# A decoder layer on one core: the residual's transposes as a stream of their own through DRAM, and two output tiles of the next token group ahead of a group's queries

## The chip, the cores and the metric

The kernel runs on one core of a Trainium2 chip. The metric is the device time of one execution in microseconds (us); lower is better.

## What is computed

One inference step of a hybrid decoder layer with model width 1024, for a prompt of 1024 tokens and 8 sample tokens (each with its own state). Cut to what matters here:

```python
def layer(x, mem, ...):                      # x: 1024 prompt tokens, and 8 sample tokens
    h = rmsnorm(x, g_mix) @ w_in             # 1024 -> 2704
    gq, gk, gv, glr, gog, rx, ry, sq, sk, sv = split_cols(h)
    o_gla = gated linear attention of gq, gk, gv       # width 384
    hr    = rglru(causal_dwconv(rx))                   # width 384, a scan over the tokens
    o_rg  = hr * gelu(ry)
    o_swa = sliding window attention of sq, sk, sv     # width 256
    x = x + concat(o_gla, o_rg, o_swa) @ w_out         # 1024 -> 1024
    q = rmsnorm(rmsnorm(x, g_x) @ w_q)                 # 1024 -> 256, queries on the memory
    x = x + softmax(q mk^T / 8) mv @ w_o               # 256 memory rows; 256 -> 1024
    return x + square(relu(rmsnorm(x, g) @ w1)) @ w2   # 1024 -> 4096 -> 1024
```

## The kernel before

Everything lies with features on the 128 partitions and tokens along the free axis, so each product reads [128 x tokens] tiles. The 1032 tokens are three groups g of 344 columns. A float32 product is made of three products of a rounded high part and the rest (XH, XL for the activations, `wh`, `wl` for the weights), so one 128 x 344 output tile over 1024 inputs is 8 terms of 3, that is 24 matmuls. XH and XL hold eight blocks; when the mixer's three outputs are ready they stand there: gated linear attention in blocks 0 to 2, the recurrence in 3 to 5, window attention in 6 and 7.

**Stages.** "In" computes the first part of h (tiles q, k and v, with the memory's keys and values `mkv` between them), "mid" the rest of it (`win`), "mem" the output product (`wo`, 8 tiles per group), the queries (`wq`, 2 tiles per group), memory attention (`mx`, `mpt`, `mpo`) and its output product (`wmo`). After them, from about 760 us to the end, come the units of the feed-forward part.

**Streams.** The mixer and memory attention are Python generators (streams). While the main line of products is written out, a planner (`pump`) inserts steps of the streams that it holds ready, at a set share of TensorE time. A stream yields what it waits for: a flag such as ("ry", g), or a slot of a pool such as "e" (two tiles of 2064 columns). `pump(lambda: ...)` in `wout` writes steps of the streams until the group's mixer outputs are flagged. A scheduler then fixes the order on each engine, and each engine works its own order in sequence.

**Recurrence.** For each group: the gates (`rgp`, 18 matmuls in all for the last group), ScalarE and VectorE work, a scan on VectorE (L655). After the last scan VectorE copies the last states (`RT`), and TensorE transposes them (`rgtp`). `ry_gen` (L684) makes gelu(ry): it takes an "e" slot for `ru`, squares on GpSimd (L687, L688), multiplies on VectorE, takes a tanh on ScalarE, and after a flag from the scan multiplies with h and writes XH and XL. Its slot comes free only as the gates of the scan let theirs go.

**Weights.** They come in pieces of 512 columns into three `ws` buffers, all by the one queue of SyncE, are rounded by ScalarE (`wh`) and subtracted by VectorE (`wl`). `feed` keeps up to three pieces staged, across the steps known at that time; `run_steps()` writes out all steps gathered up to there, so a step behind it is not staged from ahead of it.

**Residual.** x comes from DRAM with tokens on the partitions, so it must be transposed: `residual` takes a tile of 128 tokens as two pieces in `ws` buffers, transposes it on TensorE (8 of 128 x 128 through the two `psB` banks, tile `xrp`, 72 in all), and copies the result into XT, in part by ScalarE (L160), in part by VectorE (L189). It stands on the main line: 32 transposes ahead of the first group's `wo`, 24 after it and 16 after the second group's. XT then takes the output product by an addition on VectorE (L170), and the sum of squares goes through `nrm` (matmuls with a matrix of ones), a logarithm and an exponential on ScalarE and a few VectorE steps into the factor by which `mq` scales `wq`.

## Time and profile before

| what | value |
|---|---|
| median of 3 runs | 1396.29 us (1394.62 to 1396.29) |
| the profiled execution | 1393.74 us |
| its span | 1392.0 us |
| mean granted TensorE clock | 0.984 of full |
| TensorE busy | 1332.0 us (96%) |
| VectorE, ScalarE, GpSimd busy | 992.3, 691.7, 260.1 us |

The three runs are whole executions; the profiled one is a fourth, and its span leaves out 1.74 us around the recorded instructions. A row of a timeline gives the start, the duration, the engine, the line and the operation with its output and inputs, and in brackets how long the engine sat idle before it and what ended that. Rows of one form that follow each other closely are put together (x8), with the time from the first start to the last end.

### The profile page before, as it was taken

The numbers are of one execution on the slowest core, as the hardware profiler recorded it, in microseconds if no ns is written. First come the engines' busy times: TensorE is split into PE (matmuls) and PEld (weight loads), VectorE is DVE, ScalarE is ACT, GpSimd is POOL, SyncE is SP. The second block draws the span as 40 slices with busy tenths as digits, with TensorE's granted clock in tenths as the row PEclk, the third lists the DMA queues.
The fourth block names the chain that finished last, engine by engine and source line by source line (L and its number), as shares of the span: only waits on it lengthen the run. The fifth ranks groups of instructions, "written<-read, shape, count | busy, mean of one in ns | idle before, by whom it ended". The sixth has DMA issues, their size and how long they took to land.

```text
span 1392.0 us, 23667 instructions
## 1 busy us (share of the span) xinstructions
PE 1332.0 (96%) x8675; PEld 1226.1 (88%) x8675; DVE 992.3 (71%) x2097; ACT 691.7 (50%) x1439; POOL 260.1 (19%) x245
## 2 busy tenths in 40 slices
PE   6999999999997989998999999999998999999998
PEld 5889888777876877786799999999998999999997
DVE  6276787668767664767698888888766666666674
ACT  5265455245476554555566776766663222222232
POOL 3001011300003101020004232243211321321310
PEclk9999999999998899999999999999999999999999
DMA  6114010211101444442243768766689867655403
GB/s 185 46 49 122 9 49 18 67 26 31 47 8 52 140 146 128 141 133 71 71 125 109 243 223 278 251 236 214 215 308 350 309 218 244 214 188 172 158 17 106
DMA packets 197499, 198.91 MB, mean 143 GB/s; under 512 B 27938, under 2 KB 177558, under 8 KB 197368
## 3 DMA queue, kind: packets, MB, share of 16 engines
q1 hardware_dynamic: 196744, 197.11, 43.7%
q8 instruction: 68, 1.11, 0.3%
q0 software_dynamic: 640, 0.30, 0.1%
q14 instruction: 47, 0.39, 0.1%
HBM read 136.83 MB, written 61.60 MB: 143 GB/s over the span
## 4 chain that ended last, share of the span: by engine, by line
PE 81%; DVE 10%; DMA 3%; ACT 3%; issue 1%; SPq 1%; POOL 1%; DVEq 0%; ACTq 0%; POOLq 0%
PE win L140 9%; PE e L140 9%; PE fe L140 8%; PE wo L140 6%; PE c L140 4%; PE d L140 4%; PE ga L140 4%; PE fa L140 4%; PE fd L140 4%; PE f L140 2%; PE v L140 2%; PE gx L140 2%; PE b L140 2%; PE fb L140 2%; PE fc L140 2%; PE fg L140 2%
## 5 line engine op out<-in xcount | busy, mean ns | idle before, releaser
L1906 POOL TENSOR_TENSOR wsum<-wraw 128x512 f32<-128x512 f32 x60 | 82.4, 1376 | 378.4 <-DVE wop L170 285.7
L140 PE MATMUL e<-XH,wop 128*128 128x344 f32 x512 | 133.3, 322 | 4.4 <-DVE XT L170 4.4
L160 ACT ACTIVATE wop<-wraw 128x512 fp32r<-128x512 f32 x120 | 74.4, 628 | 119.9 <-PE c L140 48.8
L140 PE MATMUL win<-XL,wh 128*128 128x344 f32 x384 | 126.6, 330 | 0.0
L140 PE MATMUL win<-XH,wh 128*128 128x344 f32 x384 | 126.1, 329 | 0.2 <-ACT xy L160 0.2
L140 PE MATMUL win<-XH,wl 128*128 128x344 f32 x384 | 125.5, 327 | 0.0
L160 ACT ACTIVATE wh<-ws 128x512 fp32r<-128x512 f32 x130 | 80.2, 628 | 74.7 <-DMA ws<-in_w_out_dram 21.2
L140 PE MATMUL fe<-XH,wop 128*128 128x344 f32 x448 | 114.7, 319 | 0.0
L170 DVE TENSOR_TENSOR wop<-wraw,wop 128x512 fp32r<-128x512 f32 x120 | 86.5, 721 | 38.1 <-ACT wop L160 37.1
L170 DVE TENSOR_TENSOR wl<-ws,wh 128x512 fp32r<-128x512 f32 x130 | 91.4, 715 | 27.2 <-ACT wh L160 21.8
L160 ACT ACTIVATE wop<-wsum 128x512 fp32r<-128x512 f32 x104 | 65.6, 631 | 84.7 <-PE e L140 59.0
L170 DVE TENSOR_TENSOR wop<-wsum,wop 128x512 fp32r<-128x512 f32 x104 | 74.5, 717 | 40.2 <-ACT wop L160 39.4
L140 PEld LDWEIGHTS e<-XH,wop 128*128 128x128 f32 x512 | 91.5, 190 | 4.7 <-issue 4.7
L140 PE MATMUL e<-XL,wop 128*128 128x344 f32 x256 | 82.5, 322 | 0.0
L140 PEld LDWEIGHTS fe<-XH,wop 128*128 128x128 f32 x448 | 78.9, 188 | 0.0
L140 PEld LDWEIGHTS win<-XL,wh 128*128 128x128 f32 x384 | 72.2, 188 | 5.2 <-issue 3.9
L140 PEld LDWEIGHTS win<-XH,wl 128*128 128x128 f32 x384 | 72.3, 188 | 3.6 <-issue 2.7
L140 PEld LDWEIGHTS win<-XH,wh 128*128 128x128 f32 x384 | 72.2, 188 | 3.3 <-issue 1.9
L140 PE MATMUL fe<-XL,wop 128*128 128x344 f32 x224 | 71.4, 319 | 0.0
L160 ACT ACTIVATE hc<-hc 128x344 f32<-128x344 f32 x126 | 61.4, 488 | 19.5 <-DVE hc L170 18.1
L170 DVE TENSOR_TENSOR hst<-hc,hst 128x344 fp32r<-128x344 f32 x79 | 60.5, 767 | 13.6 <-ACT hst L160 12.4
L140 PE MATMUL wo<-XH,wh 128*128 128x344 f32 x192 | 64.0, 334 | 2.5 <-ACT wh L160 2.5
(537 smaller groups left out, 3916.7 us busy)
## 6 DMA issues: line engine op xcount, KB each, us to landing
hd<-hst SPq DMA_DIRECT2D x90, 344.0 KB
wraw<-in_ffn_w_dram SPq DMA_DIRECT2D x60, 512.0 KB
hd<-wsum SPq DMA_DIRECT2D x54, 344.0 KB
XH<-hd SPq DMA_DIRECT2D x48, 344.0 KB
XL<-hd SPq DMA_DIRECT2D x48, 344.0 KB
xoph<-hd SPq DMA_DIRECT2D x24, 344.0 KB
xopl<-hd SPq DMA_DIRECT2D x24, 344.0 KB
ws<-in_w_in_dram SPq DMA_DIRECT2D x24, 256.0 KB
```

The costliest lines, as they stand in the source:

```text
L140: PE.matmul(out, lhsT, rhs, start=start, stop=stop, **kw)
L160: return ACT.activation(out, in_, func, **kw)
L170: return DVE.tensor_tensor(out, a, b, op=op)
L1906: POOL.tensor_tensor(o, a, b, op=op)
```

## The change

Three things are edited. (1) In `ry_gen` the square moves to ScalarE and the two GpSimd steps and the VectorE product become one VectorE `stt`, with the constant 0.044715 moved into the tanh's scale. (2) `residual` is gone: a stream `x_turn` takes x in pairs of token tiles once the flag ("cum", 2) is set, transposes them, copies them back into its slot by ScalarE alone and stores them to a DRAM buffer `xd`; `x_load(g)` then loads a group's columns of XT from there with four DMAs. (3) `run_steps()` between "mid" and "mem" is gone, and two `wo` tiles of group g + 1 stand ahead of group g's queries; for the third group the `wo` tiles stand beside the `wmo` tiles of the first, two places off, and two `wmo` tiles alone ahead of its queries.

```diff
@@ -684,12 +684,10 @@
         yield [("ry", g), "e"]
         y = RY[g].rearrange("p a b -> p (a b)")
         u = T("e", G3, "ru")
-        POOL.tensor_tensor(u, y, y, op=MUL)
-        POOL.tensor_scalar(u, u, 0.044715, 1.0, op0=MUL, op1=ADD)
-        cur[0].t += 3500
-        tt(u, u, y, MUL)
+        act(u, y, AF.Square)
+        stt(u, u, 1.0 / 0.044715, y, ADD, MUL)
         yield
-        act(u, u, AF.Tanh, scale=math.sqrt(2.0 / math.pi))
+        act(u, u, AF.Tanh, scale=0.044715 * math.sqrt(2.0 / math.pi))
         stt(y, u, 1.0, y, ADD, MUL)
         release("e")
         yield [("h", g), ("free", g)]
@@ -1717,50 +1715,46 @@
         for i in range(3):
             step([win_c(c0 + 128 * i)], by_block(evac, i))
     step([win_c(1552 + 128 * i) for i in range(3)], ry_all)
-    run_steps()
-
-
-    class XBlk:
-
-        halves, cut, room = 2, 0, None
-
-        def __init__(self, t):
-            self.t, self.st = t, []
-
-        def stage(self):
-            self.st.append(T("ws", 512, "xr"))
-            h = len(self.st) - 1
-            load_x(self.t, self.st[h], slice(512 * h, 512 * h + 512))
-
+
+
+    dram = ctx.enter_context(tc.tile_pool(name="dram", bufs=1, space=bass.MemoryType.DRAM))
+    xd = dram.tile([8, 128, N], F32, name="xd")
     XTW = {}
 
-    def residual(blks):
-        b = blks[0]
-        if b.t == 0:
-            XTW["v"], XTW[4], XTW[6] = T("v", 3 * N, "XT012"), pair("XT45"), pair("XT67")
-            XT[3] = T("u", N, "XT3")
+    def x_turn():
+
+        for ts_ in ((0, 1), (2, 3), (4, 5), (6, 7), (8,)):
+            yield [("cum", 2), "e"]
+            u = v3(T("e", 2048, "xr"), 2)
+            for i, t in enumerate(ts_):
+                load_x(t, u[:, i])
+            yield 6000
+            for i, t in enumerate(ts_):
+                n = 128 if t < 8 else NS
+                for h in range(2):
+                    st = u[:, i, 512 * h:512 * h + 512]
+                    p = psB("xrp")
+                    for k in range(4):
+                        tr(p[:, k * 128:k * 128 + n], st[:n, k * 128:(k + 1) * 128])
+                    o = v3(st, 4)[:, :, :n]
+                    act(o, v3(p, 4)[:, :, :n], AF.Copy)
+                    SP.dma_start(xd[4 * h:4 * h + 4, :, tok(t)].rearrange("k p c -> p k c"), o)
+            cur[0].t += 3000
+            release("e")
+
+    def x_load(g):
+
+        if g == 0:
+            XTW[0], XTW[4], XTW[6] = v3(T("v", 3 * N, "XT012"), 3), v3(T("q", 2 * N, "XT45"), 2), v3(T("q", 2 * N, "XT67"), 2)
+            XTW[3] = v3(T("u", N, "XT3"), 1)
             NRM["p"] = T("q", 2 * G3, "nrm")
             NRM["s"], NRM["m"] = NRM["p"][:, G3:], NRM["p"][:, :G3]
-            for m in range(3):
-                XT[m] = XTW["v"][:, m * N:(m + 1) * N]
-            for m in range(4, 8):
-                XT[m] = XTW[m // 2 * 2][:, m % 2]
-        n = 128 if b.t < 8 else NS
-        c = tok(b.t)
-        for h in range(2):
-            p = psB("xrp")
-            for k in range(4):
-                tr(p[:, k * 128:k * 128 + n], b.st[h][:n, k * 128:(k + 1) * 128])
-            b.cut += 1
-            held["staged"] -= 1
-            feed()
-            pv = v3(p, 4)[:, :, :n]
-            if h == 0:
-                act(v3(XTW["v"], 3)[:, :, c], pv[:, 0:3], AF.Copy)
-                copy(XT[3][:, c], pv[:, 3])
-            else:
-                act(XTW[4][:, :, c], pv[:, 0:2], AF.Copy)
-                copy(XTW[6][:, :, c], pv[:, 2:4])
+            for m0, t in XTW.items():
+                for k in range(t.shape[1]):
+                    XT[m0 + k] = t[:, k]
+        for m0 in (0, 3, 4, 6):
+            t = XTW[m0]
+            SP.dma_start(t[:, :, gs(g)], xd[m0:m0 + t.shape[1], :, gs(g)].rearrange("m p c -> p m c"))
 
     def wout_blk(m):
         w = I["w_out"][0]
...
@@ -2233,19 +2225,27 @@
         return wcols("ffn_w1", [(0, 128 * f, 128)])
 
     phase[0] = "mem"
-    for t in TILES[0]:
-        step([XBlk(t)], residual)
-    for g in range(3):
-        side = [wmo_blk(h) for h in range(2)]
-        for m in range(8):
-            if g < 2:
-                step([wout_blk(m)], lambda blks, m=m, g=g: wout(m, g, blks[0]))
-            else:
-                step([wout_blk(m), side[m // 4]], lambda blks, m=m: (wout(m, 2, blks[0]), o_cell(0, m, blks[1])))
-        if g < 2:
-            for t in TILES[g + 1]:
-                step([XBlk(t)], residual)
-        step([wcols("mem_w_q", [(0, 128 * i, 128)]) for i in range(2)] + side[1:] * (g == 2), mem_q(g))
+    spawn(x_turn())
+    step([], lambda blks: x_load(0))
+
+    side = [wmo_blk(h) for h in range(2)]
+
+    def wouts(g, ms):
+        for m in ms:
+            step([wout_blk(m)], lambda blks, m=m: wout(m, g, blks[0]))
+
+    wouts(0, range(8))
+    for g in range(2):
+        step([], lambda blks, g=g: x_load(g + 1))
+        wouts(g + 1, range(2))
+        step([wcols("mem_w_q", [(0, 128 * i, 128)]) for i in range(2)], mem_q(g))
+        if g == 0:
+            wouts(1, range(2, 8))
+    for m in range(2, 8):
+        o = m - 2
+        step([wout_blk(m), side[o // 4]], lambda blks, m=m, o=o: (wout(m, 2, blks[0]), o_cell(0, o, blks[1])))
+    step(side[1:], lambda blks: [o_cell(0, m, blks[0]) for m in (6, 7)])
+    step([wcols("mem_w_q", [(0, 128 * i, 128)]) for i in range(2)] + side[1:], mem_q(2))
 
 
     def up_cell(i, g, more=None):
```

The count of instructions: 7976 on TensorE in both; VectorE 2099 before and 2081 after, ScalarE 1359 and 1362, GpSimd 250 and 244, SyncE 709 and 730.

The queue of SyncE where the memory's keys and values are computed, before (`ws` are pieces of weights; 1217 to 1306 are those of v):

```order
L395 DMA ws_1062<-in_mem_w_kv_dram 128x4x128
L395 DMA ws_1066<-in_mem_w_kv_dram 128x4x128
L395 DMA ws_1213<-in_mem_w_kv_dram 128x4x128
L395 DMA ws_1217<-in_w_in_dram 128x2x128 x2
L395 DMA ws_1268<-in_w_in_dram 128x2x128 x2
L395 DMA ws_1273<-in_w_in_dram 128x2x128 x2
L395 DMA ws_1306<-in_w_in_dram 128x2x128 x2
L395 DMA ws_1311<-in_w_in_dram 128x4x128
L395 DMA ws_1343<-in_w_in_dram 128x4x128
```

And after, from the piece that was 1213 on (`xr` are loads of x, `xd` the stores of its transposes; 1228, 1372 and 1377 are pieces of v's weights):

```order
L395 DMA ws_1224<-in_mem_w_kv_dram 128x4x128
L482 DMA xr_1253<-in_x_prompt_dram 128x1024
L395 DMA ws_1228<-in_w_in_dram 128x2x128 x2
L482 DMA xr_1253<-in_x_prompt_dram 128x1024
L395 DMA ws_1372<-in_w_in_dram 128x2x128
L1741 DMA xd_194<-xr_1253 128x4x128 x2
L482 DMA xr_1284<-in_x_prompt_dram 128x1024
L1741 DMA xd_194<-xr_1253 128x4x128 x2
L482 DMA xr_1284<-in_x_prompt_dram 128x1024
L1741 DMA xd_194<-xr_1284 128x4x128 x2
L395 DMA ws_1372<-in_w_in_dram 128x2x128
L395 DMA ws_1377<-in_w_in_dram 128x2x128 x2
```

Seven weight loads in a row have become loads that stand behind stores, and the stores wait for ScalarE's copies of the transposes.

VectorE at the end of "mid", behind the last scan and RT, before (xy_3749 and ru_4303 belong to the first group, whose XL the first `wo` tiles need):

```order
L170 TENSOR_TENSOR XL_84<-gg2_3102,XH_83 128x3x344
L170 TENSOR_TENSOR ru_4303<-ru_4303,xy_3749 128x1032
L170 TENSOR_TENSOR XL_84<-qS_2562,XH_83 128x2x344
L189 COPY XT3_4498<-xrp_4500 128x128
L189 COPY XT67_4497<-xrp_4509 128x2x128
L181 SCALAR_TENSOR_TENSOR xy_3749<-ru_4303,xy_3749 128x1032
L189 COPY XT3_4498<-xrp_4518 128x8
L189 COPY XT67_4497<-xrp_4527 128x2x8
L181 SCALAR_TENSOR_TENSOR xy_3749<-xy_3749 128x1032
L189 COPY XT3_4498<-xrp_4536 128x128
L170 TENSOR_TENSOR ru_4393<-ru_4393,xy_3778 128x1032
L170 TENSOR_TENSOR XL_84<-xy_3749,XH_83 128x3x344
```

And after, from the last scan on (first group: xy_3900 and ru_4462):

```order
L655 SCALAR_TENSOR_TENSOR xy_3957<-tg_4343,xy_3929,xr_4324 128x344 x3
L170 TENSOR_TENSOR wl_4660<-ws_4651,wh_4659 128x512
L189 COPY RT_102<-xy_3957 128x3
L170 TENSOR_TENSOR XL_84<-gg2_3253,XH_83 128x3x344
L170 TENSOR_TENSOR XL_84<-qS_2713,XH_83 128x2x344
L181 SCALAR_TENSOR_TENSOR ru_4462<-ru_4462,xy_3900 128x1032
L181 SCALAR_TENSOR_TENSOR xy_3900<-ru_4462,xy_3900 128x1032
L181 SCALAR_TENSOR_TENSOR xy_3900<-xy_3900 128x1032
L181 SCALAR_TENSOR_TENSOR ru_4551<-ru_4551,xy_3929 128x1032
L181 SCALAR_TENSOR_TENSOR ru_4688<-ru_4688,xy_3957 128x1032
L170 TENSOR_TENSOR XL_84<-xy_3900,XH_83 128x3x344
```

The copies of transposes are gone from between the first group's steps, and the products of `ru` for the second and third group have moved in.

TensorE about the third group's queries, before (in the middle of its first `wq` tile):

```order
L140 MATMUL nrm_6413<-rbf_5875,ones_71 128x344
L140 MATMUL nrm_6413<-nrm_4499,ones_71 128x344
L140 MATMUL wq_6433<-XH_83,wl_6349 128x344
L146 MATMUL mpt_6224<-ident_70,P_6108 128x88
L140 MATMUL wq_6433<-XH_83,wh_6348 128x344
L140 MATMUL wq_6433<-XL_84,wh_6348 128x344
L140 MATMUL wq_6433<-XH_83,wl_6349 128x344
L140 MATMUL nrm_6458<-nrm_4499,ones_71 128x344
L140 MATMUL mpo_6233<-P_6108,MKV_123 64x88 x8
L140 MATMUL wq_6467<-XH_83,wh_6422 128x344
```

And after, from the last matmul of its second `wq` tile on:

```order
L140 MATMUL wq_6454<-XH_83,wl_6379 128x344
L146 MATMUL mpt_6270<-ident_70,P_6169 128x88 x4
L146 MATMUL mpt_6279<-ident_70,P_6169 128x88 x4
L140 MATMUL nrm_6410<-rbf_5965,ones_71 128x344
L140 MATMUL nrm_6410<-nrm_4675,ones_71 128x344
L140 MATMUL nrm_6445<-nrm_4675,ones_71 128x344
L140 MATMUL mpo_6288<-P_6169,MKV_123 64x88 x8
L140 MATMUL wmo_6512<-XH_83,wh_6229 128x344
```

The three `nrm` matmuls, which stood amid the first of the two tiles of 24, now stand behind both.

Two counts from the same order: between the last `rgp` and `rgtp`, TensorE had 84 `win` matmuls before, with 17 more and then 32 `xrp` behind `rgtp`; it now has 49 `win` and 30 `wo` between them (five of the eight terms of two tiles, 6, 7, 0, 1 and 2), with no `xrp` behind. The 72 `xrp` stand among `mkv` and v of the "in" stage. The 12 loads of XT stand ahead of most of the `w_out` pieces.

## Rows read from the trace of the kernel before

**Rows 1.** The page: the span, and part 1's rows of three engines.
```profile
span 1392.0 us, 23667 instructions
...
PE 1332.0 (96%) x8675; PEld 1226.1 (88%) x8675; DVE 992.3 (71%) x2097; ACT 691.7 (50%) x1439; POOL 260.1 (19%) x245
```

**Rows 2.** Waits of TensorE: waited for, us in total, times, longest us.
```profile
PE xrp L146 <- DVE XT L189: 9.5, 5, 4.7
PE wmo L140 <- DVE mq L170: 5.4, 1, 5.4
...
PE wo L140 <- DVE wl L170: 0.9, 1, 0.9
```

**Rows 3.** Timeline of TensorE, 415 to 464 us: start, us, engine line operation.
```profile
416.08 5.44 PE L140 MATMUL rgp<-xr,gw 128*128 128x344 f32 x18
...
435.74 0.50 PE L146 MATMUL rgtp<-ident,RT 128*20 128x128 f32 x3 [1.02 <-DVE RT L189]
...
438.76 1.04 PE L146 MATMUL xrp<-ident,xr 128*128 128x128 f32 x8
...
456.04 0.66 PE L140 MATMUL wo<-XH,wh 128*128 128x344 f32 x1 [2.47 <-ACT wh L160]
...
460.89 0.32 PE L140 MATMUL wo<-XL,wh 128*128 128x344 f32 x1
...
462.30 0.32 PE L140 MATMUL wo<-XL,wh 128*128 128x344 f32 x1
```

**Rows 4.** Timeline of VectorE, ScalarE and GpSimd, 428 to 453 us.
```profile
428.61 1.24 DVE L170 TENSOR_TENSOR XL<-gg,XH 128x1032 fp32r<-128x1032 f32 x1 [0.22 <-ACT XH L160]
...
430.53 1.07 ACT L160 ACTIVATE xr<-xr 128x1032 f32<-128x1032 f32 x1
...
432.90 2.59 DVE L655 TENSOR_TENSOR_SCAN xy<-tg,xy,xr 128x344 f32<-128x344 f32 x3
...
435.63 1.91 POOL L687 TENSOR_TENSOR ru<-xy 128x1032 f32<-128x1032 f32 x1 [73.88 <-DVE xy L655]
...
437.75 2.02 DVE L170 TENSOR_TENSOR XL<-gg,XH 128x1032 fp32r<-128x1032 f32 x1 [2.06 <-ACT XH L160]
...
444.70 1.22 DVE L181 SCALAR_TENSOR_TENSOR xy<-ru,xy 128x1032 f32<-128x1032 f32 x1
...
447.59 1.06 ACT L160 ACTIVATE XH<-xy 128x1032 fp32r<-128x1032 f32 x1
...
450.00 2.07 DVE L170 TENSOR_TENSOR XL<-xy,XH 128x1032 fp32r<-128x1032 f32 x1
```

**Rows 5.** Timeline of TensorE, 489 to 502 us, about the first group's queries.
```profile
489.67 1.03 PE L146 MATMUL xrp<-ident,xr 128*128 128x128 f32 x8
...
496.11 0.74 PE L140 MATMUL nrm<-nrm,ones 128*128 128x344 f32 x2
498.04 0.42 PE L140 MATMUL wq<-XH,wh 128*128 128x344 f32 x1 [1.18 <-ACT wh L160]
...
501.78 0.32 PE L140 MATMUL wq<-XH,wh 128*128 128x344 f32 x1
```

**Rows 6.** Timeline, 643 to 657 us, about the third group's queries.
```profile
643.33 0.84 PE L140 MATMUL nrm<-rbf,ones 128*128 128x344 f32 x2
...
644.79 0.52 DVE L177 TENSOR_SCALAR nrm<-nrm 128x344 f32<-128x344 f32 x1 [1.43 <-PE nrm L140]
...
645.40 0.48 ACT L164 ACTIVATE rbf<-nrm 128x344 f32<-128x344 f32 x1
...
650.09 2.04 DVE L181 SCALAR_TENSOR_TENSOR XT<-XT,PRM,rbf 128x344 f32<-128x344 f32 x4
...
650.61 0.31 PE L140 MATMUL wq<-XH,wl 128*128 128x344 f32 x1
...
652.04 1.80 DVE L170 TENSOR_TENSOR XL<-XT,XH 128x344 fp32r<-128x344 f32 x4
...
655.63 0.94 DVE L170 TENSOR_TENSOR mq<-wq,nrm 128x344 f32<-128x344 f32 x2
...
656.29 0.63 PE L140 MATMUL wmo<-XH,wh 128*128 128x344 f32 x1 [5.36 <-DVE mq L170]
```

**Rows 7.** The chain that ended last, 127 to 132 us: start, us, what.
```profile
127.23 0.64 ACT wh L160
...
127.90 0.70 DVE wl L170
...
128.62 3.17 DMA ws<-in_w_in_dram
```

More of the change, by code (lines that the diff above doesn't have):

```diff
@@ L1866, in cells @@
         return [ap[:, i * GW:(i + 1) * GW] for i in range(ap.shape[1] // GW)]
-    dram = ctx.enter_context(tc.tile_pool(name="dram", bufs=1, space=bass.MemoryType.DRAM))
     hd = [dram.tile([18, 128, 2 * GW], F32, name=f"hd{c}") for c in range(NUNIT)]
-    xd = dram.tile([8, 128, N], F32, name="xd")
     ST, HC, PL = {}, {}, {}
```

## The prediction

> **What bounds the kernel now.** The page comes first: TensorE is busy 1332.0 us of a span of 1392.0 [rows 1]. The change keeps every matmul, so at most 60 us of waits are there to be taken, and some of those lie at the start, which it doesn't touch. The view of TensorE's waits then says which of them have to do with the residual: 9.5 us in five waits of `xrp` for the copies out of its two banks, and beside them 5.4 us of `wmo` for `mq` and 0.9 of `wo` for `wl` [rows 2]. The timeline shows where they are: most between 438.76 and 460.89, at the boundary between "mid" and "mem" [rows 3], some around the first group's queries [rows 5]; the 5.4 us stand behind the third group's queries [rows 6]. A second cost hides in the same rows: after a wait the matmuls come more slowly. From 456.04 to 460.89 TensorE starts 16 `wo` matmuls, 0.30 us each; from 460.89 to 462.30 it starts 9 in 1.41 us, 0.157 each [rows 3]. That is the clock's lower level after an idle stretch, against its higher one, and for these 16 matmuls it costs 16 x 0.145 = 2.3 us.
>
> **The boundary.** What it costs before: 438.76 to 460.89 is 22.1 us. In it are 32 transposes at 0.13 (8 take 1.03 [rows 5]), 4.1 us, and 16 matmuls that would take 2.5 at full clock. The other 15.5 are loss, and with them go `rgtp`'s wait of 1.0 [rows 3] and the 0.9 of `wo` [rows 2]: 17.4 us.
>
> It looks as if all of it went with the transposes. But TensorE also waits here for something else, which the transposes happened to fill. The first group's XL, which the last three terms of each `wo` tile need, was written at 450.00 to 452.07 [rows 4], at the end of this chain: last `rgp` (ends at 421.5 [rows 3]), gates, exponential on ScalarE (430.53), last scan (432.90 to 435.49), `ru`, tanh, two `stt`, XH (447.59), XL [rows 4]. That is 30.5 us from the end of `rgp`. In the new order it goes: 14.8 us from the end of `rgp` to the end of the scan (14.0 before; ScalarE has more ahead of the exponential, which I put at 0.8), RT and `rgtp` 1.5 (0.2 and 0.5, and handing over), the copy out of it 0.5, a square at 1.06 as XH's row, `stt` 1.22, tanh 1.06, two `stt` 2.44, XH 1.06, XL 1.24 [rows 4], and some 0.2 for each of seven hand-overs: 26.3 us. Behind the last `rgp` TensorE has 49 `win` and 30 `wo` matmuls, 79 x 0.157 = 12.4 us, and `rgtp` 0.5. It then stands still for 13.4 us, and pays about the same 2.3 of slow clock afterwards: 15.7 against 17.4, **a gain of 1.7 us**. The transposes have gone to a place where TensorE has no wait to fill and cost their full time there; the sum of work is the same, and only waits count. Lower bound of the chain: with no hand-overs and no delay ahead of the exponential it is 24.1, a gain of 3.9; upper bound: the 30.5 of before, a loss of 2.5.
>
> One price in this chain hangs on GpSimd. The copy into XL of 128 x 1032 took 1.24 us while GpSimd was idle, and 2.02 and 2.07 where its `ru` steps ran at the same time [rows 4]; I take 1.24, since the change takes GpSimd out. The Trainium skill has a rule for it ("SBUF — State Buffer", Who interferes with whom): a VectorE instruction with two SBUF inputs contends with a GpSimd instruction that reads SBUF, and the later one is blocked. The two rows agree with it; by rows alone, without the rule, the 2.07 would stay and the boundary's gain fall to 0.9. The three removed rounds of GpSimd steps cost nothing elsewhere: TensorE waited for none of them.
>
> **The first group's queries.** From 489.67 to 501.78 are 12.1 us [rows 5]. In them: 24 transposes 3.1, `nrm` 0.6, 13 `wq` matmuls 2.0; the other 6.4 us are waits for copies, for x, for `wh`, and slow clock. Now two `wo` tiles stand there, 48 matmuls or 7.5 us, whose weights are staged ahead and whose XH and XL are written; they cover the sum of squares of the group before, and there is nothing to wait for. But `nrm` now stands between the two `wq` tiles instead of ahead of them: the steps from it to `mq` have 24 matmuls (3.8 us) for cover and take some 4.6 (0.52 the first, one round on ScalarE 0.5 + 0.5, then VectorE with `wl` among it), so 0.8 is given back: **a gain of 5.6**. The second group's 16 transposes show no wait of their own; nothing is gained there.
>
> **The third group's queries.** Before, `nrm` at 643.33 was ahead of 24 of the 48 `wq` matmuls; `wq` ended at 650.8, and `mq` came at 655.63, since VectorE did four `stt` (0.49 each) and four XL (0.43 each) of the next stage first [rows 6]. Now `nrm` stands behind all 48 and 8 `mpt`. From the end of `wq`: `mpt` and `nrm` 1.4, the first VectorE step twice 1.0, logarithm and exponential with handing over 1.2 (0.48 each [rows 6]), then by the new order 18 VectorE instructions up to the first `mq`, at 0.46 a piece 8.3: 11.9 us. TensorE does 2.2 us of `mpt`, `nrm` and `mpo` in it, so it stands still for 9.7 instead of 5.4: **a loss of 4.3**. If VectorE is free of half of them by then, the loss is 0.2; if weight copies stand among them too, 6.
>
> **The "in" stage.** No row of before shows this stall, since x was not there. SyncE's queue runs in order. In it the loads of v's weights now stand behind stores which wait for ScalarE's copies. For one such load the path from the transposes is: transposes 1.0, two copies of the size of `wh` 2 x 0.64, the load 3.17, `wh` 0.64, `wl` 0.70 [rows 7], 6.8 us; TensorE has between some 45 matmuls of `mkv` and v for the first of them, and some 30 matmuls and 16 transposes for the second, 4 to 6 us. I take **a loss of 1.0**, with 0 below (all in time) and 5 above (both late by 2 to 3). [...] ScalarE's 18 more copies, 10 us, fall into a stretch in which it is half idle (50% over the span [rows 1]); the 12 loads of XT come long before `wo` is added to it. Were that cover gone, TensorE's `wo` would wait a load's 3 us.
>
> **Sum.** -1.7 - 5.6 + 4.3 + 1.0 = -2.0 us. Against the profiled execution's 1393.74 us, which is its span and 1.74 around it, that is 1391.7. The runs' median stands 2.55 above that execution, so the forecast for a median is **1394.3 us**. That is within 0.2% (2.8 us) of before, which is about what a measurement of this kernel can tell from no change.
>
> **Rivals.**
> (a) *A clear gain*: the third group's gap doesn't grow. For it: VectorE sat idle 1.43 us just before `nrm` there [rows 6], so it may have done part of the 18 steps in time; against it: XL of the next stage hangs on `nrm` itself. Then -6.3 us, 1390.0; with the short chain at the boundary too, 1387.8.
> (b) *Slower*: the single queue holds up v's weights. Place: the two pieces of weights behind the stores of the second and the fourth pair of tiles. Price: 6.8 us of path against cover of only about 2 if x itself lands late, 4.8 for each, 9.6, and in place of the 1.0 that makes +6.6, 1402.9. It decides from 5.8 us of stall on. For it: x comes in 512 KB, two or four at a time, and the sequence store, load, store repeats; against it: `mkv` runs for 12 us there.
> (c) *No change at all*: the boundary wait belongs wholly to the recurrence, and the chain is as long as before in all but name; then the boundary is 0 to +0.8, the sum near 0, 1396.
>
> **Chances.** The forecast 0.4 (its own range 1391 to 1397.5), (a) 0.2, (b) 0.2, (c) 0.2. The forecast lies by two fifths below 1393.5, (a) nearly all; the forecast's other part and (c) are within 0.2%; (b) and a corner of (c) above. So faster 0.40, within 0.2% 0.37, slower 0.23. The range reaches from rival (a) with the shorter chain to a little short of (b)'s full price: 1386 to 1402.
>
> **What would show it.** No `xrp` wait at 438 to 456, but one wait of 10 to 15 us of `wo` for XL or XH of the recurrence shortly after 450, with the clock low behind it; two `wo` tiles where the first group's `wq` waited, and no wait there over 1 us; a `wmo` wait for `mq` of 8 to 11 us near 660; waits of v for `wl` or `wh` of some tenths to 2 us at 125 to 150. The forecast is wrong if the boundary's wait is under 5 us (the chain is shorter or better covered than I make it), if `wmo`'s stays at 5, or if v or `xrp` waits over 5 us in the "in" stage.

## The result and the profile after

The changed kernel takes 1417.49 us (median of 4 runs, 1413.27 to 1419.28) against 1396.29 of the kernel before (4 runs, 1394.62 to 1396.44): a ratio of 1.0155 [1.0134, 1.0176]. That is slower by 1.6%, and above the range of the forecast. Its profiled execution took 1419.28 us with a span of 1417.6, 25.6 more than before.

First the page of the changed kernel: the span, the engines, and the granted TensorE clock in 40 slices.

```profile
span 1417.6 us, 23674 instructions
...
PE 1347.3 (95%) x8675; PEld 1243.0 (88%) x8675; DVE 977.3 (69%) x2079; ACT 694.6 (49%) x1442; POOL 255.8 (18%) x239
...
PEclk9999799999999897999899999999999999999999
```

TensorE does the same 8675 recorded instructions as in [rows 1] and is busy 15.3 us longer with them. So most of the loss isn't idle time: the same matmuls are slower. The low digits of the clock stand in the slices of 142 to 177, 461 to 496, 532 to 567 and 673 to 709 us. The view of TensorE's waits answers to [rows 2]:

```profile
PE wmo L140 <- DVE mq L170: 8.5, 1, 8.5
PE wo L140 <- ACT XH L160: 7.5, 1, 7.5
...
PE wo L140 <- DVE mq L170: 2.9, 1, 2.9
...
PE rgtp L146 <- DVE RT L189: 2.1, 1, 2.1
...
PE gx L140 <- DVE gt L902: 2.1, 1, 2.1
```

The `xrp` waits are gone. In their place stand waits for XH of the recurrence and for `mq`, as the prediction had them, and no wait of v or `xrp` over 5 us. The timeline of TensorE places them (answering to [rows 3, 5, 6]; a bracket is the idle time before):

```profile
152.80 0.28 PE L140 MATMUL v<-wh,XL 128*128 128x256 f32 x1
...
161.23 0.41 PE L140 MATMUL v<-wh,XL 128*128 128x256 f32 x1
...
201.32 0.43 PE L140 MATMUL win<-XH,wh 128*128 128x344 f32 x1
...
474.20 0.50 PE L146 MATMUL rgtp<-ident,RT 128*20 128x128 f32 x3 [2.13 <-DVE RT L189]
482.22 0.94 PE L140 MATMUL wo<-XH,wh 128*128 128x344 f32 x2 [7.52 <-ACT XH L160]
484.55 0.65 PE L140 MATMUL wo<-XL,wh 128*128 128x344 f32 x1 [1.39 <-DVE XL L170]
...
527.03 0.32 PE L140 MATMUL wq<-XH,wl 128*128 128x344 f32 x1
530.25 0.63 PE L140 MATMUL wo<-XH,wh 128*128 128x344 f32 x1 [2.91 <-DVE mq L170]
...
680.41 0.62 PE L140 MATMUL wmo<-XH,wh 128*128 128x344 f32 x1 [8.47 <-DVE mq L170]
```

The first `win` of "mid" starts at 201.32; before, that was this row:

```profile
179.97 0.32 PE L140 MATMUL win<-XH,wh 128*128 128x344 f32 x1
```

So TensorE is 21.4 us late when "mid" begins; 9.4 of these are the 72 transposes, which now stand there and are saved later. The same landmarks in both traces divide TensorE's time. "Work" is what the stretch gained or gave up in transposes (0.13 each) and `wo` matmuls (0.157), and in the six `nrm` and sixteen `mpo` matmuls that now stand behind the third group's `wq` (669.19 to 671.95, with the end of the `mpt` ahead of them about 3 us); the loss is the rest.

| stretch, from landmark to landmark | before, us | after, us | work moved | loss |
|---|---|---|---|---|
| first `mkv` to first `win` of "mid" | 62.9 | 83.4 | +9.4 | +11.1 |
| to the end of the last `win` | 258.9 | 266.1 | 0 | +7.2 |
| to the end of the first group's `wq` | 68.7 | 60.0 | -7.3 +7.5 | -8.9 |
| to the end of the third group's `wq` | 143.3 | 140.3 | -7.5 -2.1 -3 | +9.6 |
| to the end of the last `f` matmul ahead of the `fa` tiles | 94.8 | 102.6 | +3 | +4.8 |

The losses sum to 23.8; 0.8 comes ahead of the table and about 1 behind it. Now the largest, by the view of windows. Columns: window, its length, then busy us and instructions of TensorE, weight load, VectorE, ScalarE and GpSimd; granted clock; DMA share; GB/s. Before:

```profile
120.00:140.00 20.00, 19.47 (x181) 18.12 (x180) 13.29 (x26) 12.25 (x29) 0.74 (x1) 1.00 0.58 145
140.00:160.00 20.00, 19.04 (x199) 17.44 (x199) 14.42 (x36) 7.73 (x16) 0.00 (x0) 1.00 0.05 15
160.00:180.00 20.00, 19.60 (x195) 17.47 (x194) 16.36 (x54) 8.74 (x18) 2.39 (x2) 1.00 0.02 5
```

After:

```profile
120.00:140.00 20.00, 18.31 (x168) 17.33 (x166) 7.45 (x14) 10.72 (x23) 0.00 (x0) 1.00 0.96 289
140.00:160.00 20.00, 17.29 (x149) 15.51 (x150) 6.89 (x15) 7.21 (x15) 0.97 (x1) 0.76 0.74 226
160.00:180.00 20.00, 20.00 (x139) 17.73 (x140) 12.63 (x31) 8.02 (x21) 0.00 (x0) 0.81 0.25 55
```

Three columns tell it. The DMA engines are nearly full (0.96) where they were at 0.58. VectorE is busy about half as long as before until 160. And TensorE, which is busy for most of the time, gets 0.76 and 0.81 of its clock from 140 to 180. An estimate from these rows: the missing clock is 0.24 x 20 + 0.19 x 20 = 8.6 us, and the added idle time of the first two windows is 4.4 - 1.5 = 2.9; together 11.5, about the 11.1 of the table. In finer windows the clock is at 0.50 from 142.5 to 145 and from 157.5 to 162.5 and at 1.00 from 147.5 to 155, so 0.76 is a mean of its two levels, 1.2 and 2.4 GHz. No single wait is long; the longest one at the place is in the timeline of all engines, 153 to 164 us:

```profile
154.61 1.75 PE L140 MATMUL gx<-E 48*64 48x64 f32 x40
...
156.40 0.38 ACT L160 ACTIVATE gt<-gx 64x256 f32<-64x256 f32 x1 [3.46 <-PE gx L140]
...
157.42 0.89 DVE L902 COPY_PREDICATED gt<-mk,gx 128x256 f32<-128x256 uint8 x2
...
158.46 0.69 PE L140 MATMUL gx<-E 48*128 48x64 f32 x4 [2.11 <-DVE gt L902]
```

These are linear attention's small products: 40 matmuls in 1.75 us, a round over ScalarE and VectorE with nothing of v to fill it, and the next four. After it v's matmul at 161.23 takes 0.41 where the one at 152.80 took 0.28.

The traffic by the DMA view, 120 to 165 us, after:

```profile
DMA packets 14434, 10.55 MB, mean 235 GB/s; under 512 B 1624, under 2 KB 13400, under 8 KB 14432
...
xr<-in_x_prompt_dram SPq DMA_DIRECT2D x8, 512.0 KB
xd<-xr SPq DMA_DIRECT2D x16, 256.0 KB
```

Before, it was 3.20 MB at 71 GB/s. The stream reads 4 MB and writes 4 MB within these 45 us.

### The profile page after: what moved, and what is told of

It is laid out like the page before. It is cut to its first block, busy times and chain, and to the rows that moved or that the text cites. A ratio compares the mean times of both kernels' runs of the same rounds, so it can differ in the third digit from the quotient of the medians.

```text
span 1417.6 us, 23674 instructions
## 1 busy us (share of the span) xinstructions
PE 1347.3 (95%) x8675; PEld 1243.0 (88%) x8675; DVE 977.3 (69%) x2079; ACT 694.6 (49%) x1442; POOL 255.8 (18%) x239
## 4 chain that ended last, share of the span: by engine, by line
PE 78%; DVE 10%; ACT 4%; DMA 3%; issue 2%; POOL 1%; SPq 1%; DVEq 0%; ACTq 0%; POOLq 0%
PE win L140 9%; PE e L140 9%; PE fe L140 7%; PE c L140 4%; PE wo L140 4%; PE d L140 4%; PE ga L140 4%; PE fa L140 4%; PE fd L140 4%; PE v L140 3%; PE gx L140 2%; PE b L140 2%; PE fb L140 2%; PE fc L140 2%; PE fg L140 2%
## 5 line engine op out<-in xcount | busy, mean ns | idle before, releaser
L1898 POOL TENSOR_TENSOR wsum<-wraw 128x512 f32<-128x512 f32 x60 | 86.8, 1448 | 375.3 <-DVE wop L170 316.2
L170 DVE TENSOR_TENSOR hst<-hc,hst 128x344 fp32r<-128x344 f32 x79 | 58.7, 744 | 11.7 <-ACT hst L160 10.6
```

Source lines behind the costliest of these rows:

```text
L170: return DVE.tensor_tensor(out, a, b, op=op)
L1898: POOL.tensor_tensor(o, a, b, op=op)
```

## The experiments

Three questions: what each part of the change is worth alone, what in the moved stream costs the 20 us, and whether a better place exists. Every ratio is to the kernel before, run on the same chip; its median there lies between 1394.41 and 1396.29, so variants are compared by their ratios. Diffs are cut with `...`.

**The parts alone.** The square on ScalarE, on the kernel before:

```diff
-        POOL.tensor_tensor(u, y, y, op=MUL)
-        POOL.tensor_scalar(u, u, 0.044715, 1.0, op0=MUL, op1=ADD)
...
-        tt(u, u, y, MUL)
+        act(u, y, AF.Square)
+        stt(u, u, 1.0 / 0.044715, y, ADD, MUL)
...
```

> The kernel before with only the square moved from GpSimd to ScalarE. It takes GpSimd's steps of up to 3 us and the slowed VectorE copies out of the chain ahead of the first XL, but the transposes still stand there: 1395 us, within 2 of before, by every theory; over 5 us faster would mean that the chain and not the transposes bounded the boundary.

Measured: 1390.87 us (1388.14 to 1392.13), 0.9966 [0.9953, 0.9979]. It is faster than before by more than expected, and the fastest kernel of the study. Its waits of TensorE, against [rows 2], begin with:

```profile
PE xrp L146 <- DVE XT L189: 5.9, 6, 1.5
```

And its timeline, against [rows 3, 4]:

```profile
446.25 1.22 DVE L170 TENSOR_TENSOR XL<-xy,XH 128x1032 fp32r<-128x1032 f32 x1
...
452.80 0.65 PE L140 MATMUL wo<-XH,wh 128*128 128x344 f32 x1 [3.82 <-ACT wh L160]
```

XL is written in 1.22 instead of 2.07, VectorE comes to its copies of transposes sooner, `xrp` waits 5.9 instead of 9.5, and the first `wo` starts at 452.80 instead of 456.04. The same edit undone in the changed kernel:

```diff
-        act(u, y, AF.Square)
-        stt(u, u, 1.0 / 0.044715, y, ADD, MUL)
+        POOL.tensor_tensor(u, y, y, op=MUL)
+        POOL.tensor_scalar(u, u, 0.044715, 1.0, op0=MUL, op1=ADD)
...
+        tt(u, u, y, MUL)
...
```

> The changed kernel with the square of the gelu back on GpSimd. If the recurrence's chain alone sets the wait at the boundary in the changed kernel (my forecast), the chain gets GpSimd's steps and slowed copies back, about 5 us as the kernel before lost by them: 1422 us. If the boundary has another bound: 1417 us.

Measured: 1421.02 (1420.59 to 1424.81), 1.0196 [1.0179, 1.0213], by the ratios 5.7 us above the changed kernel. So the edit is worth some 5 to 6 us in either.

The steps joined, on the kernel before:

```diff
-    run_steps()
```

> The kernel before with only run_steps() between the middle and the memory stage removed. x and then w_out can be staged from ahead of the boundary; the first wo waited 2.5 us for wh there, but the recurrence's XL comes at 452 us anyway: 1395 us, within 2 of before. Over 4 us faster would mean that the staging bounded the boundary.

Measured: 1395.66, 1.0009 [0.9998, 1.0019]: nothing. The order of `wo` and queries, on the kernel before, with the transposes still on the main line:

```diff
...
+        for t in TILES[g + 1]:
+            step([XBlk(t)], residual)
+        wouts(g + 1, range(2))
         step([wcols("mem_w_q", [(0, 128 * i, 128)]) for i in range(2)], mem_q(g))
+        if g == 0:
+            wouts(1, range(2, 8))
...
```

> The kernel before with only the new order of wo and queries; the residual's transposes stay on the main line, each group's ahead of its first wo tile. If the two wo tiles in front of the first group's queries are what takes its wait away (my forecast), 5 us are gained there, and some 4 lost behind the third group's queries and 3 to 6 after the first ones, where wo waits for mq: 1398 us, within 3. If the transposes alone made that wait: 1400 to 1404 us.

Measured: 1400.5 (1399.27 to 1403.0), 1.0049 [1.0032, 1.0066]. Its waits:

```profile
PE xrp L146 <- DVE XT L189: 9.8, 5, 4.7
PE wmo L140 <- DVE mq L170: 8.5, 1, 8.5
...
PE wo L140 <- ACT wh L160: 5.0, 3, 2.5
```

The 8.5 of the third group's gap come with the order, and the order alone gains nothing at the first queries: the transposes' waits are still there, and behind them `wo` now waits 2.5 us for weights. The old order in the changed kernel:

```diff
...
-        wouts(g + 1, range(2))
...
-        step([wcols("mem_w_q", [(0, 128 * i, 128)]) for i in range(2)], mem_q(g))
+        step([wcols("mem_w_q", [(0, 128 * i, 128)]) for i in range(2)] + side[1:] * (g == 2), mem_q(g))
...
```

> The changed kernel with all wo tiles of a group ahead of its queries and none of the next, as before; the stream through DRAM, the removed run_steps and the gelu on ScalarE stay. Theory 3 (the order makes the loss after the first queries, 6.6 us, and in the third group's gap, 7.3 us): those go, the first group's queries lose some 3 us again, about 1407 us. Theory 1: the order gives about as much as it takes, 1417 us within 3.

Measured: 1416.94 (1413.97 to 1419.75), 1.0152 [1.013, 1.0174]. Within the changed kernel the order is worth nothing: what the two `wo` tiles cover at the first queries is given back by the longer `wmo` wait (8.5 against 6.8) and by `wo` behind `mq` (2.9 against 1.8). So the loss lies in the stream.

**What of the stream costs the time.** First the transposes and copies left out (64 of the 72 transposes and their 16 copies; the last, short token tile keeps its own; x is stored untransposed), the data movement kept:

```diff
-                    for k in range(4):
-                        tr(p[:, k * 128:k * 128 + n], st[:n, k * 128:(k + 1) * 128])
-                    act(o, v3(p, 4)[:, :, :n], AF.Copy)
...
```

> The changed kernel whose stream x_turn only moves data: its loads and stores stay, 64 of the 72 transposes and 16 of their 18 copies are left out, so x goes to XT untransposed. Theory 1 (the copies on ScalarE stand ahead of linear attention's own, TensorE waits for those chains, and the clock falls): 8.3 us of transposes go and some 9 us of waits and slow clock with them, about 1400 us, and the clock stays at its upper level from 135 to 175 us. Theory 2 (weights of v wait behind the stores on SyncE's queue): the queue still holds the same loads and stores, only the 8.3 us go, about 1409 us. Theory 3 (the two wo tiles ahead of the queries make the loss): 1409 us too.

Measured: 1411.18 (1409.69 to 1411.72), 1.011 [1.0094, 1.0125]. The first stretch still takes 80.8 us, though 64 transposes (8.3 us) are gone: a loss of 16.9. A window of it:

```profile
140.00:160.00 20.00, 17.32 (x107) 13.84 (x107) 6.14 (x13) 3.21 (x8) 0.00 (x0) 0.50 0.72 202
```

With less work the clock falls even further. So the loss doesn't need the transposes and their copies; what remains is the loads and stores. Is it that the weights queue behind the stores, as rival (b) had it? The stores issued by ScalarE instead:

```diff
-                    SP.dma_start(xd[4 * h:4 * h + 4, :, tok(t)].rearrange("k p c -> p k c"), o)
+                    ACT.dma_start(xd[4 * h:4 * h + 4, :, tok(t)].rearrange("k p c -> p k c"), o)
```

> The changed kernel with the 18 stores of the transposes issued from ScalarE, right behind the copies that they wait for, so that no weight load stands behind them on SyncE's queue. Theory 2 (the stores hold up v's weights, TensorE runs short of work and its clock falls): the 11 us lost in the first stage beyond the transposes' own time shrink to some 3, and the clock stays up from 135 to 175 us: about 1408 us. Theory 1 (the copies on ScalarE stand ahead of linear attention's own): the copies are still there, 1416 us.

Measured: 1416.35 (1412.77 to 1417.59), 1.0152 [1.0134, 1.017]; first stretch 81.6. So the loss doesn't need the stores in SyncE's queue. The run is no clean swap, though: more than a third of the rows of TensorE's order in this stretch differ from the changed kernel's, and the transposes now wait for x, which there took 0.6 us:

```profile
PE xrp L146 <- DMA xr<-in_x_prompt_dram: 4.5, 3, 2.8
```

What speaks against (b) more plainly is the changed kernel itself, where TensorE waits for v's weights only this long:

```profile
PE v L140 <- ACT wh L160: 1.0, 1, 1.0
```

Now without the stores (XT is loaded from the prompt as it lies):

```diff
-                    SP.dma_start(xd[4 * h:4 * h + 4, :, tok(t)].rearrange("k p c -> p k c"), o)
...
```

> The changed kernel without the 18 stores of x's transposes: x_load reads the same amount of other data from the input, so XT holds wrong values. Theory 4 (loads and stores together, 8.4 MB, fill the 16 DMA engines from 120 to 160 us, v's weights and x land late, TensorE runs dry and its clock falls): half the bytes are gone, the 11 us of the first stage beyond the transposes' own time shrink to 4 or less and v no longer waits for wh: 1409 us. Theory 1 (the copies on ScalarE): nothing gained, 1417 us.

Measured: 1400.69 (1397.23 to 1403.13), 1.0038 [1.0026, 1.0051]. More comes back than expected: the first stretch takes 75.2, a loss of 2.9 beside the transposes, "mid" is shorter too (260.4 for 265.7), and the clock from 140 to 160 is 0.91:

```profile
140.00:160.00 20.00, 19.77 (x205) 17.54 (x204) 12.24 (x26) 9.29 (x24) 0.74 (x1) 0.91 0.28 68
```

With a quarter of each store's bytes (XT comes from the prompt as it lies here too):

```diff
-                    SP.dma_start(xd[4 * h:4 * h + 4, :, tok(t)].rearrange("k p c -> p k c"), o)
+                    SP.dma_start(xd[4 * h:4 * h + 1, :, tok(t)].rearrange("k p c -> p k c"), o[:, :1])
...
```

> The changed kernel with each of the 16 large stores cut to a quarter of its bytes (one block of four), at the same places of the queue; as without stores, XT is loaded from the input and holds wrong values. If the bytes on the DMA engines are the cost, nearly as much goes as without stores, 1404 us. If the number of stores on the queue and the waits of the slots for them are, 1414 us.

Measured: 1401.73 (1399.26 to 1404.74), 1.0046 [1.003, 1.0062]; first stretch 76.1, a loss of 3.8. The loss goes with the bytes, not with the number of stores. But with fewer bytes the scheduler also sets another order: about a third of the rows of TensorE's order in this stretch differ, as they do without stores. So these two runs don't tell whether the bytes act through traffic on the chip or through the order. The same bytes in runs of 2 KB, read back by 44 loads:

```diff
+    xw = dram.tile([9, 2, 128, 512], F32, name="xw")
-                    SP.dma_start(xd[4 * h:4 * h + 4, :, tok(t)].rearrange("k p c -> p k c"), o)
+                    SP.dma_start(v3(xw[t, h][:, :4 * n], 4), o)
...
```

> The changed kernel with the stores of x's transposes laid out in DRAM so that each partition writes one run of 2 KB instead of four of 512 B; the loads of XT become 44 smaller ones. The bytes stay, and the order on TensorE in the first stage too. If the number of small packets makes the traffic slow, some 8 of the first stage's 11 us go, about 1409 us. If it is the bytes, 1417 us; if the stores' mere place ahead of the slot's release, 1417 us as well.

Measured: 1414.48 (1407.96 to 1417.16), 1.0132 [1.0103, 1.0162]. From 120 to 165 us there are 8286 packets instead of 14434 for the same 10.6 MB, and v waits less for `wh` (0.4 at most, for 1.0). TensorE's order in the stretch is that of the changed kernel, and the stretch takes the same 83.4 us, with a slow clock again:

```profile
160.00:180.00 20.00, 20.00 (x127) 17.48 (x127) 13.00 (x32) 7.23 (x19) 0.00 (x0) 0.74 0.21 47
```

So the number of packets isn't it: same order, same bytes, same loss.

**Another place.** The stream spread over "mid", by a wait of the planner between the loads and the slot:

```diff
-            yield [("cum", 2), "e"]
+            yield [("cum", 2)]
+            yield 45000
+            yield ["e"]
```

> The changed kernel with the five pairs of token tiles 45 us apart in the planner's time instead of one after the other, over both stages. Theory 4 (the DMA engines): 2 MB per 45 us leave the engines free for the weights, the first stage's 11 us and the middle stage's 5 go: 1402 us. If the transposes' place among linear attention's small products or the copies on ScalarE were the cost, half of it would stay: 1410 us.

Measured: 1429.54 (1425.92 to 1432.09), 1.0248 [1.0223, 1.0272], the slowest of all, and outside both expectations. The windows show something else:

```profile
285.00:295.00 10.00, 10.00 (x56) 7.25 (x55) 1.93 (x5) 1.51 (x4) 0.00 (x0) 1.00 0.37 100
295.00:305.00 10.00, 10.00 (x32) 3.80 (x31) 0.00 (x0) 0.46 (x1) 0.00 (x0) 0.51 0.00 0
305.00:315.00 10.00, 10.00 (x32) 3.86 (x30) 0.00 (x0) 0.00 (x0) 0.00 (x0) 0.50 0.01 2
315.00:325.00 10.00, 10.00 (x38) 6.43 (x37) 2.15 (x5) 3.13 (x10) 0.00 (x0) 0.50 0.07 15
325.00:335.00 10.00, 10.00 (x61) 7.81 (x61) 5.31 (x29) 1.06 (x2) 0.00 (x0) 0.95 0.29 59
```

For 30 us TensorE runs at half clock without a pause in its busy time, while the DMA engines are nearly idle. What it did there is in its timeline of 294 to 296 us: small products of window attention, two at a time, between single `win` matmuls.

```profile
294.31 0.33 PE L140 MATMUL sgx<-sg 48*8 48x96 f32 x2
...
295.18 0.59 PE L140 MATMUL win<-XH,wh 128*128 128x344 f32 x1
```

The planner counts the stream's time against the share of the other streams and may make it up later; the same with that time credited back:

```diff
             yield 45000
             yield ["e"]
...
+            pace["credit"] += 1100 * len(ts_)
```

> As the spread stream, and the TensorE time of the transposes isn't charged to the streams' share, so that the recurrence isn't put off by them. Theory 5 (at the boundary TensorE waits for the recurrence's chain, and its last gates come later by what the transposes took of the share): some 7 us of the 11 us of waits there go, about 1397 us if the spreading works as expected. Without that link: as the spread stream.

Measured: 1403.15 (1396.03 to 1404.91), 1.0045 [1.0026, 1.0064]. The long half clock is gone, and 26 us with it, of which the 30 us at half clock account for about 15 (an estimate from the windows). So the planner's order made the long low stretch. (The profiled execution took 1398.73, below the median; the waits given further down are from it.) The stream from the flag of the output gate on, late in "mid":

```diff
-            yield [("cum", 2), "e"]
+            yield [("gog", 0), "e"]
```

> The changed kernel whose stream x_turn waits for the flag of the first output gate instead of the decay sums, so that all its transposes stand among the win matmuls of the middle stage. Theory 1 (interplay with linear attention in the first stage): the 12 us lost between mkv and the return to win go, some is given back in the middle stage, about 1405 us. Theory 2 (the queue): in the middle stage one weight block is needed every 11 us, the queue has time, about 1405 us too; a wait of win for wh of over 1 us would speak for it. Theory 3 (the order of wo and queries): 1417 us.

Measured: 1407.12 (1405.59 to 1409.18), 1.0083 [1.0066, 1.01]. The first stretch is back at 62.8 us, but `rgtp` waits 7.9 ahead of the boundary's 7.5:

```profile
PE rgtp L146 <- DVE RT L189: 7.9, 1, 7.9
```

The loads and stores themselves do little here. They now pass from 380 to 420 us, where the DMA engines are nearly as full as they were in the first stage, and TensorE waits 2.6 us for x once, but the clock stays up:

```profile
380.00:400.00 20.00, 17.12 (x116) 15.92 (x115) 6.10 (x10) 10.18 (x17) 0.00 (x0) 1.00 0.89 274
400.00:420.00 20.00, 20.00 (x89) 15.26 (x90) 2.96 (x3) 11.52 (x22) 0.00 (x0) 0.91 0.58 178
```

"Mid" takes 271.3 us, which beside the 9.4 of the transposes is some 2 us more than in the kernels that change only what comes later (260.0 to 260.3). So the same bytes beside `win` matmuls don't cost the 11 us of the first stage.

The same with the credit given back:

```diff
-            yield [("cum", 2), "e"]
+            yield [("gog", 0), "e"]
...
+            pace["credit"] += 1100 * len(ts_)
```

> The kernel with the late stream, its transposes not charged to the streams' share. If the recurrence is put off by that charge (theory 5), the wait of rgtp of 7.9 us falls to 2 or less and the wait of wo for XH from 7.5 to 5: about 1399 us against 1407. Without that link 1407 us.

Measured: 1408.62 (1407.4 to 1410.69), 1.0102 [1.0084, 1.0121]. That was a miss: here the credit doesn't help, `rgtp` waits 13.8:

```profile
PE rgtp L146 <- DVE RT L189: 13.8, 1, 13.8
```

The stream behind v, at the start of "mid":

```diff
-            yield [("cum", 2), "e"]
+            yield [("v", 8), "e"]
```

> The changed kernel whose stream x_turn waits for the last tile of v instead of the decay sums: the same loads, stores, copies and transposes start some 50 us later, among the first win matmuls, and 82 win and 6 wo matmuls are left between the last gates and rgtp instead of 49 and 30. If the first stage's order and traffic are the cost (11 us, with the clock low from 140 to 172 us): v ends at 180 us as before, the loss goes, and the boundary's waits fall from 11 to about 6, as with 72 and 12 matmuls in the spread stream: 1400 us. If the round trip costs the same wherever it stands: 1412 us or more.

Measured: 1398.91 (1395.48 to 1402.43), 1.0029 [1.0016, 1.0041]: by the ratios 17.6 us less than the changed kernel, by one flag, though still slower than before. The first stretch takes 64.0, and the windows look much like those of before:

```profile
120.00:140.00 20.00, 19.48 (x183) 18.37 (x182) 13.50 (x25) 12.40 (x29) 0.54 (x1) 1.00 0.74 197
140.00:160.00 20.00, 19.06 (x188) 17.55 (x187) 12.94 (x33) 6.21 (x13) 0.19 (x1) 0.91 0.19 67
160.00:180.00 20.00, 19.62 (x194) 17.90 (x194) 16.00 (x54) 9.57 (x19) 2.29 (x2) 1.00 0.00 2
```

Last, no stream: on the kernel before, with the square moved, the later groups' transposes woven between the `wo` tiles of the group before.

```diff
+                if m % 2 and m // 2 < len(TILES[g + 1]):
+                    step([XBlk(TILES[g + 1][m // 2])], residual)
...
```

> The kernel before with the gelu on ScalarE, and the second and third group's transposes woven on the main line between the wo tiles of the group before (one token tile after every second wo tile) instead of in a block ahead of the queries. Nothing goes by DRAM, the order of wo and queries is that of before. If the first group's queries wait only because the copies out of two banks can't keep up with transposes in a block, the 6.4 us there go but for what wh costs: 1386 us against the 1390.9 of the gelu alone. If the sum of squares ahead of the queries is the real bound: 1391 us.

Measured: 1411.83 (1410.85 to 1415.72), 1.0128 [1.0108, 1.0148], a miss: x's pieces now take their `ws` buffers between the weights of the `wo` tiles, and `wo` waits for weights 11.1 us instead of 3.8.

```profile
PE wo L140 <- ACT wh L160: 11.1, 4, 4.0
```

The boundary can be compared over five of these runs. Between the last `rgp` and `rgtp` stand so many matmuls, and behind it so much waiting:

| kernel | `win` + `wo` there | `rgtp` + XH + XL waits, us |
|---|---|---|
| stream behind v | 82 + 6 | 1.1 + 4.7 + 1.8 = 7.6 |
| stream spread, credited | 72 + 12 | 1.0 + 4.0 + 1.1 = 6.1 |
| changed kernel | 49 + 30 | 2.1 + 7.5 + 1.4 = 11.0 |
| stream late | 15 + 30 | 7.9 + 7.5 + 1.4 = 16.8 |
| stream late, credited | 0 + 3 | 13.8 + 7.5 + 1.4 = 22.7 |

In the main, the less cover the planner leaves behind the last `rgp`, the longer TensorE stands still (the first two rows are the exception). From the changed kernel down, 34 and 42 matmuls less, or 5.3 and 6.6 us at 0.157, add 5.8 and 5.9 us of waiting: the wait belongs to the recurrence's chain, and the transposes had only been standing in it.

## Why the prediction was wrong

**The failed step** is the term of the "in" stage, "a loss of 1.0 (0 to 5)". It measured 11.1. The forecast asked only whether v's weights come in time, and they nearly did: v waits 1.0 once for `wh`, and its sign "v or `xrp` waits over 5 us" didn't come. What it didn't ask is what 8 MB of traffic do to a stage that had moved 3.2 MB, and what TensorE then has left to run: linear attention's small products stand without enough of v between them (as from 154.61 to 158.46), the engine idles for 3 us in short pieces, and its clock is at 0.76 and 0.81 for 40 us. It counted the clock behind the boundary's wait (2.3 us) but not here. Rival (b) had the place and nearly the size (9.6), but not the mechanism: it asked for two waits of 4.8 for late weights, and TensorE waited 1.0; and with the stores out of SyncE's queue the stretch takes 81.6 all the same. That its size came close is luck.

**"Mid"** was put at nothing and lost 7.2, or 8.2 with the 1.0 of `rgtp`'s wait that had stood in this stretch. Some 1.5 of it is scatter: it took 258.6 us in the one profile of before, from the first `win` to the start of the last, but 260.0 to 260.3 in the three kernels that change only what comes later or the square. In the kernels whose first stretch is full of the stream's loads and stores and has the transposes it took 265.6 (old order, square on GpSimd, 2 KB runs) to 267.4; without the stores or with thin ones 260.4 and 260.6. But with the transposes left out it took 262.7, though the first stage's loss was there in full. In the changed kernel the clock is at 0.83 from 280 to 300 and at 0.91 from 400 to 420, where it was 1.00 before: an estimate of 0.17 x 20 + 0.09 x 20 = 5.2 of the 7.2. What sets this order isn't shown.

**The boundary** was right in its mechanism and too small: "a gain of 1.7", with 3.9 as the best case. The one wait of 10 to 15 us came as three: behind the end of the last `win` (467.4) they are 2.13, 7.52 and 1.39, and 15 matmuls lose 2.2 to the clock (0.29 each instead of 0.157 for most): 13.2 against 17.4, a gain of 4.2. From the last `rgp` (ends at 459.6) to the end of XL (484.5) it was 24.9 us for the 26.3 assumed. XL took 1.23 for the 1.24 taken, so the row of idle GpSimd was the right one, and the kernel with the square alone shows the same 1.22.

**The first queries** are the second failed term: "a gain of 5.6" from 6.4 less 0.8. The 6.4 are there (6.5 with the 12 `wq` matmuls that start from 498.04 to 501.78, where the forecast counted 13): no wait from 519.07, where `wq` starts, to its end at 527.3. The 0.8 to be given back were 2.9 in a wait of `wo` for `mq`, and some 6.7 more up to the end of the third group's `wq`, in which the clock stands at 0.73 (520 to 540), 0.84 (540 to 560) and 0.87 (640 to 660): about 9.6 in all. Nothing is left of the gain, as the run with the old order shows from the other side.

**The third group's queries** came out nearly as forecast: a stand-still of 9.7 for 5.4, measured 8.47 and 0.87 ahead of `nrm` for 5.36. From the end of `wq` (667.7) to the first `mq` (679.8) it is 12.1 us for the 11.9 of the sum. The cause is shown, since the order alone brings it. The stretch lost about 4.8 for the 4.3; slow clock behind the stand-still is there in both kernels (0.86 from 660 to 680 before, 0.76 from 680 to 700 after).

By parts, then: the square about -5 us, the joined steps 0, the order +7 on the kernel before but about 0 inside the changed one, and the stream, with what it takes from the order's gain, the rest: about +26. Behind v it costs about +9, which is still more than the square brings. The terms of the forecast were nearly all waits. But of the 25.6 us TensorE is idle for 10.3 and busy for 15.3 more, with the same instructions: more than half of the loss is matmuls that ran slowly.

**What stays open.** The loss in the "in" stage goes with the bytes that are moved there. Whether they slow the stage through contention on the chip, or because the scheduler, which reckons with these transfers, puts the products into an order that leaves the small ones bare, isn't separated: without stores or with thin ones the order changed too, and the run that changed only the packets kept both order and time. Two runs bear on it. The late stream moved the same bytes at a clock of 1.00 and 0.91, so traffic alone doesn't bring the clock down; and the spread stream lost the clock for 30 us with the DMA engines nearly idle, so an order of products alone can. But with the stores on ScalarE's queue, in another order, TensorE waited 4.5 us for x itself, so late transfers can cost time too. A run with the bytes of the changed kernel in the order that the one without stores has, or the reverse, wasn't made.

## What to carry to other kernels

Work that stands in another step's wait costs little there and its full price where it is moved to, so ask first whose wait it fills. Price a moved stream by its bytes and by what its new stage has beside it, not only by the waits of the weights behind it: here one flag later was worth some 18 us. And after each wait that a change adds, count the slow matmuls behind it; with TensorE busy 95% of the time, they were the larger half of the loss.

## What the hardware showed that was not expected

TensorE's clock fell to half, 1.2 GHz, while the profile shows the engine without any idle time: 30 us in the spread stream's run at 0.51 and 0.50 granted and 10.00 of 10 us busy, and up to 320 us what it ran was pairs of small 48 x 96 products between single `win` matmuls. So in this run a TensorE that the profile shows as busy didn't keep the higher level.

VectorE's slow-down beside GpSimd reaches the smallest copy too. In the kernel with the square back on GpSimd, GpSimd's `ru` step ran from 470.52 to 472.63, and VectorE's copy of 128 x 3, issued in it, took 1.90 us, to the end of that step; in the changed kernel, with GpSimd idle, the same copy took 0.17 (third row):

```profile
470.52 2.11 POOL L687 TENSOR_TENSOR ru<-xy 128x1032 f32<-128x1032 f32 x1 [81.11 <-DVE xy L655]
470.75 1.90 DVE L189 COPY RT<-xy 128x3 f32<-128x3 f32 x1
...
473.98 0.17 DVE L189 COPY RT<-xy 128x3 f32<-128x3 f32 x1
```

The Trainium skill ("SBUF — State Buffer", Who interferes with whom) says that copies, too, can take the pair of ports that VectorE shares with GpSimd, and that the engine which comes second waits for the whole instruction. This row agrees with it.
